# Mixer output projection: plain tiles against Strassen's seven half-size products

## Chip, cores and metric

One core of one Trainium2 chip (trn2) runs the whole kernel. The metric is device time in microseconds of one execution; the time before is 785.6 us, the median of three runs.

## What is computed

The reference is one layer of a hybrid decoder trunk on 512 tokens of width 1024. What matters here is the step that closes the token mixer, and its neighbours:

```python
h = rmsnorm(x, mix_norm)
z = h @ w_in
y_a = pool_mixer(z_pool, w_pool, pool_scale) @ w_branch_a
y_b = spatial_gating(z_uv, ...) @ w_branch_b
x = x + (sigmoid(z_gate_a) * y_a + sigmoid(z_gate_b) * y_b) @ w_out
h = rmsnorm(x, ffn_norm)
x = x + conv_ffn(h, w_up, conv_w, conv_b, w_down)
```

`w_out` is 1024 x 1024. The mixed operand, called `ga` in the kernel, is 512 x 1024, so the projection is 512 x 1024 times 1024 x 1024. The change rewrites this one product.

## The kernel before

**Three matmuls for one.** Every fp32 operand is cut into a rounded part and a rest, both in the type fp32r, and each product of a 128 x 128 and a 128 x 512 block is three matmuls: high by high, high by low, low by high (`mm3`, lines 201 to 205). Activations are cut by `split` (ScalarE copies the high part, VectorE subtracts the rest: lines 235 and 236). Weights are cut by `parts` (line 68 on ScalarE, line 69 on VectorE) from a raw block of 128 x 1024 that a DMA on SP's queue has loaded.

**Weights in a queue.** `plan` and `plan_seven` put units (a load and a cut) in the list `todo`. `take` (line 154) hands the next cut unit to the matmuls and first prepares further ones, so that two more stay ready (`AHEAD`), with loads up to four units further (`LOADS`). The cut pairs live in two rings of four buffers (`wp`). Raw weights, activations' pairs and the residual all share one pool of 37 blocks of 4 KB per partition (`blk`). Instructions are emitted in program order and then scheduled, so on an engine they may stand in another order than in the text.

**Two ways to multiply.** `by_token` (line 407) is the plain way: for one half `fh` of the output columns, four PSUM banks (one for each block of 128 tokens) collect the eight blocks of the contraction; a unit of weights serves 24 matmuls of 512 columns. `seven` (line 347) is Strassen's way, in Winograd's form: token halves, contraction halves and column halves give seven products instead of eight, each of 24 matmuls here, in two units of 12. Its stationary operands are the blocks A11, A12, A22 and four combinations D, S2, S3 and E. `combine` (line 333) makes these with four VectorE subtractions or additions of 256 columns, and `halves` and `cut_into` cut them. The weights' combinations are made in `plan_seven`: by VectorE on the raw block (`adds="vector"`), by accumulating DMAs on POOL's queue, or by both (`"some"`). Three sets of weights of the input projection and the down projection go this way already; the latter in three parts with the order `DOWN`.

**Around the change.** The branch product of `yp` with `w_a` runs by `by_token` for `fh` 0 and 1 (lines 571 to 576). After each half, VectorE multiplies the four banks by the gate (line 575) and adds `gb` (line 576); that gives `ga`. Then the residual `x` (line 581) and the embedding input `pt` (line 587) are loaded on ScalarE's DMA queue, and `pt` is split. Then TensorE turns all eight channel tiles of `ga`: four transposes of 128 x 128 per tile, through the identity, into one bank (`turned`, line 614), and each is split into `m`. `by_token(m, ...)` with `w_o` runs for both halves; VectorE adds the result to `x` (line 626) and ScalarE squares it (line 604). Then 24 matmuls embed `pt` (`embed`), while the norm (line 599 on POOL, line 649 on VectorE) is made, and TensorE turns the normed rows `xn` for the up projection.

Of the kernel before, what the change touches and what calls it, by code (L numbers as in the profile page):

```python
# [7 lines left out]
F32 = mybir.dt.float32  # L8
F32R = mybir.dt.float32r
AF = mybir.ActivationFunctionType  # L10
ALU = mybir.AluOpType
PSUM = bass.MemoryType.PSUM

P = 128
T = 512
H = T // 2
D = 1024
KD = D // P
NT = T // P
FF = 2816  # L20
KF = FF // P
# [5 lines left out]
AHEAD = 2  # L27
# [3 lines left out]
HK = KD // 2  # L31
# [3 lines left out]
DOWN = ("P1", "P5", "P2", "P6", "P7", "P4", "P3")  # L35
# [9 lines left out]
def trunk(ctx, tc, xT, xr, pT, wsT, par, bsp, w_u0, w_u1, w_v, w_ga, w_gb, w_p, w_pl,  # L45
# [6 lines left out]
    small = ctx.enter_context(tc.tile_pool(name="small", bufs=2))  # L52
# [4 lines left out]
    V, S, G, PE = nc.vector, nc.scalar, nc.gpsimd, nc.tensor  # L57

    def block(name, shape=(2, T), dtype=F32):
        return blk.tile([P, *shape], dtype, tag="blk", name=name)  # L60


    def parts(raw, cols=CW, first=False, spare=False):

        pool, th, tl = (blk, "blk", "blk") if spare else (wp, "hi", "lo")
        hi = pool.tile([P, CW], F32R, tag=th, name="whi")
        lo = pool.tile([P, CW], F32R, tag=tl, name="wlo")
        (V.tensor_copy if first else S.copy)(hi[:, :cols], raw[:, :cols])  # L68
        V.tensor_tensor(lo[:, :cols], raw[:, :cols], hi[:, :cols].bitcast(F32), op=ALU.subtract)  # L69
        return hi, lo  # L70
# [3 lines left out]
    todo = []  # L74
# [3 lines left out]
    def load_raw(src):  # L78
        raw = block("raw", (CW,))
        n = src.shape[-1]  # L80
        nc.sync.dma_start(raw[:, :n], src)
        return raw
# [5 lines left out]
    def plan(src, cols=CW, **kw):  # L88
        got = []
        todo.append((lambda: got.append(load_raw(src)), lambda: parts(got[0], cols, **kw)))  # L90
# [56 lines left out]
    def prepare(loads=LOADS):  # L147
        while todo and len(loaded) < loads:
            load, cut = todo.pop(0)
            load()  # L150
            loaded.append(cut)
        ready.append(loaded.pop(0)())

    def take(ahead=AHEAD, loads=LOADS):
        while (todo or loaded) and len(ready) <= ahead:
            prepare(loads)
        return ready.pop(0)

    flat = "p k f -> p (k f)"
# [19 lines left out]
            plan_map(i // 5)  # L179
    for i in range(KD):  # L180
        plan(w_a[i // 4, i % 4].rearrange(flat))
    for i in range(KD):
        plan(w_o[i // 4, i % 4].rearrange(flat))
    for k in range(2):
        plan(w_ple[k])
    done_at = {q0 + n: (q0, n) for q0, n in PARTS}
# [14 lines left out]
    def mm3(o, w, a, first, last, **kw):  # L201
        (wh, wl), (ah, al) = w, a
        PE.matmul(o, wh, ah, start=first, stop=False, **kw)  # L203
        PE.matmul(o, wh, al, start=False, stop=False, **kw)  # L204
        PE.matmul(o, wl, ah, start=False, stop=last, **kw)  # L205

    def wslice(c, j, n=P):
        return c[0][:, j * n:(j + 1) * n], c[1][:, j * n:(j + 1) * n]

    def act(b, sl=slice(None)):  # L210
        return b[:, 0, sl], b[:, 1, sl]

    def work(name):
        return tmp.tile([P, T], F32, tag="work", name=name, bufs=8)

    def bank():
        return ps.tile([P, T], F32, tag="mm", name="mm")
# [9 lines left out]
    def split(src, scale=None):  # L227

        b = block("blk", (2, T), F32R)
        split_into(b, src, scale)  # L230
        return b
# [18 lines left out]
    def col(c, i):  # L250
        return pr[:, c + i:c + i + 1]
# [9 lines left out]
    ident = const.tile([P, P], F32, name="ident")  # L261
# [59 lines left out]
    seeded = [psb.tile([P, T], F32, tag=f"sd{n}", name="sd") for n in range(2)]  # L321
# [82 lines left out]
        for f in fill:  # L404
            f()

    def by_token(acts, fh, banks, kps, between=None):

        for kp in kps:
            c = take()  # L410
            for b in range(NT):
                for kk in range(2):
                    k = 2 * kp + kk
                    mm3(banks[b], act(acts[k], slice(b * P, (b + 1) * P)), wslice(c, kk, T), k == 0, k == KD - 1)


    x2 = []
    x = []
# [12 lines left out]
    for k in range(KD):  # L431
        if k + 1 < KD:
            load(k + 1)
        b = split(x[k], col(C_MIX, k))
        c = take(1, 1)
# [87 lines left out]
    ga = gate(X, [nothing] * 3 + [(lambda f=f: head(f)) for f in range(HEADS)])  # L523
# [22 lines left out]
    yp = []  # L546
# [11 lines left out]
    for i in range(KD):  # L558
        pooled.append(pool(i))
        fh = i // 4  # L560
        if i % 4 == 0:
            banks = [bank(), bank(), *seeded]
# [5 lines left out]
            group_maps(i // 5)  # L568


    for fh in range(2):
        banks = [bank() for _ in range(NT)] if fh == 0 else [bank(), *seeded, bank()]
        by_token(yp, fh, banks, range(KD // 2))
        for b in range(NT):
            V.tensor_tensor(ga[b][:, fh], banks[b], ga[b][:, fh], op=ALU.mult)
            V.tensor_tensor(ga[b][:, fh], ga[b][:, fh], gb[b][:, fh], op=ALU.add)

    x = [block("x") for _ in range(NT)]
# [23 lines left out]
    def squares(b, fh, sums):  # L602
        sq = work("sq")
        S.activation(sq, x[b][:, fh], AF.Square, accum_out=sums[b][:, fh:fh + 1])

    def columns(z, b, f):

        return z[b][:, f // HK, f % HK * P:(f % HK + 1) * P]

    def turned(z, f):  # L610

        tp = bank()
        for b in range(NT):
            PE.transpose(tp[:, b * P:(b + 1) * P], columns(z, b, f), ident)  # L614
        return tp


    m = []
    for f in range(KD):
        m.append(split(turned(ga, f)))  # L620
    xss = [small.tile([P, 2], F32, tag="xss", name="xss", bufs=NT) for _ in range(NT)]
    for fh in range(2):
        banks = [bank() for _ in range(NT)] if fh == 0 else [*seeded, bank(), bank()]
        by_token(m, fh, banks, range(KD // 2))
        for b in range(NT):
            V.tensor_tensor(x[b][:, fh], banks[b], x[b][:, fh], op=ALU.add)
            squares(b, fh, xss)


    c_ple = [take(), take()]  # L630
# [30 lines left out]
    xss = [small.tile([P, 2], F32, tag="xss", name="xss", bufs=NT) for _ in range(NT)]  # L661
# [11 lines left out]
    for i in range(KF):  # L673
        if i:
            o1, o2 = proj8(xg), proj8(xg)
        else:

            o1, o2 = bank(), bank()
            c = [take(), take()]
# [3 lines left out]
        a = conv(2 * i, o1)  # L683
        S.activation(a, a, AF.Gelu)
        b = conv(2 * i + 1, o2)
        V.tensor_tensor(a, a, b, op=ALU.mult)
        if i % 2 == 0:
            q = i // 2
# [5 lines left out]
        else:  # L694
            z = split(a)
# [3 lines left out]
        if part:  # L699
            q0, n = part  # L700
# [31 lines left out]
    for b in (2, 3, 0, 1):  # L732
        th, j = divmod(b, 2)
# [9 lines left out]
        n = 0  # L743
        for group in groups:
            for k in range(KD):
                a = XE[th][k % HK][:, k // HK]
                a = [a[:, z, j * P:(j + 1) * P] for z in range(2)]
                for ob, c0 in group:
                    mm3(ob, a, [z[:, c0:c0 + ob.shape[-1]] for z in wg[k]], k == 0, k == KD - 1)
            for ob, c0 in group:  # L750
                w = ob.shape[-1]
                fh, c1 = divmod(c0, T)
# [22 lines left out]
def _layout(i):  # L775

    import numpy as np

    a = {k: np.asarray(v) for k, v in i.items()}

    def ft(w):
        K, F = w.shape
        return w.reshape(K // P, P, F // P, P).transpose(2, 1, 0, 3)

    def th(w):
        return w.reshape(KD // 2, 2, P, 2, T).transpose(3, 0, 2, 1, 4)

    def sv(w):
        return w.reshape(2, HK, P, 2, T).transpose(0, 3, 1, 2, 4).reshape(4, HK, P, T)

    def cols(v):
        return v.reshape(-1, P).T

    w_in = a["w_in"][0]
    up = ft(a["w_up"][0])
    cw, cb = a["conv_w"][0], a["conv_b"][0]

    def pairs(z):
        return np.stack([z[:KF], z[KF:]], 1).reshape(z.shape)

    cwt = pairs(cw.T.reshape(2 * KF, P, 3)).transpose(1, 0, 2).reshape(P, -1)
    cbt = pairs(cb.reshape(2 * KF, P)).T
    par = np.concatenate([cols(a["mix_norm"][0]), cols(a["pool_scale"][0]), cols(a["sgu_norm"][0]),
                          cols(a["ffn_norm"][0]), cols(a["ple_norm"][0]), cwt, cbt], 1)
    o = {
        "xT": a["x"][0].T.reshape(KD, P, T),
        "xr": a["x"][0].reshape(NT, P, D),
        "pT": a["p"][0, 0].T.reshape(2, P, T),
        "wsT": a["w_spatial"][0].transpose(2, 0, 1),
        "par": par,  # L810
        "bsp": a["b_spatial"][0],
        "w_u0": w_in[:, D:D + T].reshape(KD, P, T),
        "w_u1": ft(w_in[:, D + T:2 * D]),
        "w_v": sv(w_in[:, 2 * D:3 * D]),
        "w_ga": sv(w_in[:, 3 * D:4 * D]),
        "w_gb": sv(w_in[:, 4 * D:]),
        "w_p": ft(w_in[:, :D]),
        "w_pl": a["w_pool"][0].reshape(2, 2, 2, P, 256).transpose(0, 3, 1, 2, 4),
        "w_a": th(a["w_branch_a"][0]),
        "w_b": th(a["w_branch_b"][0]),  # L820
        "w_o": th(a["w_out"][0]),
        "w_up": pairs(up),

        "w_dn": a["w_down"][0].reshape(KF // 2, 2, P, 2, T).transpose(1, 3, 0, 2, 4).reshape(4, KF // 2, P, T),
        "w_g": a["w_ple_gate"][0].reshape(KD, P, D),
        "w_ple": a["w_ple"][0].reshape(2, P, D),
        "gfin": a["final_norm"],
    }
    return {k: np.ascontiguousarray(o[k]) for k in _ORDER}
# [14 lines left out]
```

## Time and profile before

| | before |
|---|---|
| median of 3 runs (lowest, highest) | 785.6 us (785.59, 786.09) |
| the profiled execution: its own time | 787.91 us |
| the profiled execution: span from first to last instruction | 786.2 us |
| TensorE busy | 771.4 us (98%) |
| VectorE busy | 547.2 us (70%) |
| ScalarE busy | 372.9 us (47%) |
| POOL busy | 42.8 us (5%) |
| DMA moved | 95.35 MB, 121 GB/s over the span |

Busy time of TensorE is modelled to the end of each matmul, and matmuls overlap, so the distance from start to start is what one costs. "PEld" is the loading of stationary weights, which runs beside the matmuls. A bracket behind a row gives the idle time just before it and what ended that. The chain that ended last is followed back from the last instruction, at each step to what released it.

### The profile page before, as it was taken

How to read it: one execution, taken by the hardware profiler on the slowest of the kernel's cores; microseconds unless marked ns; L12 is line 12 of the kernel's file. 1: busy time of each engine (PE TensorE's matmuls, PEld its weight loads, DVE VectorE, ACT ScalarE, POOL GpSimd, SP SyncE). 2: the span in 40 equal slices, each digit the busy share in tenths (PEclk: the TensorE clock that was granted, in tenths of full speed). 3: DMA queues.
4: the chain of work that ended last, by engine and by line, in shares of the span. 5: the costliest groups of instructions: out<-in, count | busy, mean ns of one | idle time of the engine just before them, and what ended most of it. 6: DMA issues, size and time to landing. Idle time of an engine off the chain costs nothing.

```text
span 786.2 us, 9275 instructions
## 1 busy us (share of the span) xinstructions
PE 771.4 (98%) x3482; PEld 637.8 (81%) x3482; DVE 547.2 (70%) x769; ACT 372.9 (47%) x538; POOL 42.8 (5%) x79
## 2 busy tenths in 40 slices
PE   9999999999999999999999999999999999999896
PEld 7888878888888888788888888888888888877785
DVE  7797898866576744536577678666668767788655
ACT  6576736582241322335544545534445434457623
POOL 0000200000112100001000010000000011000100
PEclk9999999999999999999999999999999999999999
DMA  9712225124031508102841344822425664310311
GB/s 350 270 55 81 80 81 188 54 103 166 28 127 62 214 29 324 49 0 76 325 103 37 102 108 132 289 91 51 108 82 133 232 170 111 117 54 31 130 55 54
DMA packets 36829, 95.35 MB, mean 121 GB/s; under 512 B 3376, under 2 KB 3504, under 8 KB 36784
## 3 DMA queue, kind: packets, MB, share of 16 engines
q1 hardware_dynamic: 32192, 84.68, 30.7%
q0 software_dynamic: 3008, 5.77, 4.7%
q10 hardware_dynamic: 1584, 4.31, 1.5%
q8 instruction: 27, 0.44, 0.2%
q14 instruction: 18, 0.15, 0.1%
HBM read 91.60 MB, written 3.15 MB: 121 GB/s over the span
## 4 chain that ended last, share of the span: by engine, by line
PE 89%; DVE 4%; DMA 2%; ACT 2%; issue 1%; POOL 0%; POOLq 0%; SPq 0%; ACTq 0%; DVEq 0%
PE mm L203 24%; PE mm L204 23%; PE mm L205 23%; PE sd L204 6%; PE sd L203 6%; PE sd L205 6%; DVE wlo L69 1%; ACT whi L68 1%; DMA pt<-in_pT 1%; DMA raw<-in_w_g 1%; PE mm L498 1%; DVE raw L137 1%; PE mm L614 0%; DMA x<-in_xT 0%; DVE xn L649 0%
## 5 line engine op out<-in xcount | busy, mean ns | idle before, releaser
L69 DVE TENSOR_TENSOR wlo<-raw,whi 128x1024 fp32r<-128x1024 f32 (+1 forms) x186 | 217.9, 1179 | 158.2 <-ACT whi L68 157.8
L68 ACT CAST whi<-raw 128x1024 fp32r<-128x1024 f32 (+1 forms) x179 | 183.7, 1031 | 214.7 <-PE mm L204 56.8
L203 PE MATMUL mm<-blk,whi 128*128 128x512 f32 x480 | 186.4, 390 | 0.6 <-ACT blk L238 0.6
L204 PE MATMUL mm<-blk,whi 128*128 128x512 f32 x480 | 186.7, 389 | 0.0
L205 PE MATMUL mm<-blk,wlo 128*128 128x512 f32 x480 | 186.6, 389 | 0.0
L203 PEld LDWEIGHTS mm<-blk,whi 128*128 128x128 f32 x480 | 90.0, 188 | 19.9 <-ACT blk L238 0.7
L205 PEld LDWEIGHTS mm<-blk,wlo 128*128 128x128 f32 x480 | 90.1, 188 | 18.9
L204 PEld LDWEIGHTS mm<-blk,whi 128*128 128x128 f32 x480 | 90.1, 188 | 18.5
L203 PE MATMUL mm<-whi,blk 128*128 128x512 f32 x214 | 83.7, 391 | 1.4 <-DVE xe L239 1.4
L204 PE MATMUL mm<-wlo,blk 128*128 128x512 f32 x214 | 83.4, 390 | 0.0
L205 PE MATMUL mm<-whi,blk 128*128 128x512 f32 x214 | 83.3, 389 | 0.0
L203 PEld LDWEIGHTS mm<-whi,blk 128*128 128x128 f32 x214 | 40.2, 188 | 10.1 <-issue 1.8
L205 PEld LDWEIGHTS mm<-whi,blk 128*128 128x128 f32 x214 | 40.2, 188 | 8.4
L204 PEld LDWEIGHTS mm<-wlo,blk 128*128 128x128 f32 x214 | 40.2, 188 | 8.1
L203 PE MATMUL sd<-whi,blk 128*128 128x512 f32 x110 | 43.1, 392 | 0.3 <-ACT u L367 0.3
L204 PE MATMUL sd<-wlo,blk 128*128 128x512 f32 x110 | 42.8, 389 | 0.0
L205 PE MATMUL sd<-whi,blk 128*128 128x512 f32 x110 | 42.8, 389 | 0.0
L137 DVE TENSOR_TENSOR raw<-raw 128x1024 f32<-128x1024 f32 (+1 forms) x36 | 42.0, 1199 | 0.1
L203 PE MATMUL sd<-whi,cmb 128*128 128x512 f32 x92 | 36.2, 395 | 0.8 <-ACT u L367 0.8
L204 PE MATMUL sd<-wlo,cmb 128*128 128x512 f32 x92 | 36.1, 392 | 0.8 <-DVE wlo L69 0.8
L205 PE MATMUL sd<-whi,cmb 128*128 128x512 f32 x92 | 35.8, 389 | 0.0
L205 PE MATMUL mm<-whi,cmb 128*128 128x512 f32 x92 | 35.8, 389 | 0.0
(167 smaller groups left out, 1047.9 us busy)
## 6 DMA issues: line engine op xcount, KB each, us to landing
raw<-in_w_up SPq DMA_DIRECT2D x44, 512.0 KB, 4.3
raw<-in_w_dn SPq DMA_DIRECT2D x25, 512.0 KB, 3.5
raw<-in_w_dn POOLq DMA_DIRECT2D x10, 512.0 KB, 6.0
raw<-in_w_v SPq DMA_DIRECT2D x8, 512.0 KB, 11.3
raw<-in_w_ga SPq DMA_DIRECT2D x8, 512.0 KB, 4.0
raw<-in_w_gb SPq DMA_DIRECT2D x8, 512.0 KB, 3.7
raw<-in_w_p SPq DMA_DIRECT2D x8, 512.0 KB, 4.7
raw<-in_w_b SPq DMA_DIRECT2D x8, 512.0 KB, 3.9
```

The costliest lines, as they stand in the source:

```text
L68: (V.tensor_copy if first else S.copy)(hi[:, :cols], raw[:, :cols])
L69: V.tensor_tensor(lo[:, :cols], raw[:, :cols], hi[:, :cols].bitcast(F32), op=ALU.subtract)
L137: V.tensor_tensor(z[:, :cols], z[:, :cols], raw[extra, ch][:, :cols], op=ALU.add)
L203: PE.matmul(o, wh, ah, start=first, stop=False, **kw)
L204: PE.matmul(o, wh, al, start=False, stop=False, **kw)
L205: PE.matmul(o, wl, ah, start=False, stop=last, **kw)
L498: PE.matmul(mx[:, n * P:(n + 1) * P], vt[n].rearrange("p a t -> p (a t)")[:, f * P:(f + 1) * P], wsm[:, f, :], start=True, stop=True)
```

## The change

The output projection goes by `seven`, with the accumulating DMAs making all the weights' combinations (`adds="all"`) and the cut units of the products P1 and P5 placed in the block pool instead of the rings (`spare`). The operand is turned by pairs of channel tiles (`turn_pair`): two tiles are transposed into two banks, one is copied to SBUF, and the blocks and combinations for one contraction step are made from both. Pairs 0 and 1, which need only the first half of `ga`, are turned after the second and third unit of the second half of the branch product; pairs 2 and 3 after it. There, `take` keeps three, then four units ready instead of two. `w_o` is laid out like `w_dn`.

```diff
-    for i in range(KD):
-        plan(w_o[i // 4, i % 4].rearrange(flat))
+    todo.extend(plan_seven(blocks(w_o), DOWN, "all", spare=("P1", "P5")))
...
-    def by_token(acts, fh, banks, kps, between=None):
-
+    def by_token(acts, fh, banks, kps, ahead=AHEAD, after=()):
+
+        after = list(after)
         for kp in kps:
-            c = take()
+            c = take(ahead)
             for b in range(NT):
                 for kk in range(2):
                     k = 2 * kp + kk
                     mm3(banks[b], act(acts[k], slice(b * P, (b + 1) * P)), wslice(c, kk, T), k == 0, k == KD - 1)
+            if after:
+                after.pop(0)()
...
+    m = []
+    m11 = []
+
+    def turn_pair(q):
+        tp, s2 = turned(ga, 2 * q), turned(ga, 2 * q + 1)
+        s1 = work("s1")
+        S.copy(s1, tp)
+        if q % 2 == 0:
+            m11.append(block("a11", (2, 2, H), F32R))
+        t = m11[-1][:, q % 2]
+        cut_into(t, s1[:, :H])
+        z = split(s2)
+        m.append(dict(A11=t, A12=z[:, :, :H], A22=z[:, :, H:], **combine(s1, s2)))
+
     for fh in range(2):
         banks = [bank() for _ in range(NT)] if fh == 0 else [bank(), *seeded, bank()]
-        by_token(yp, fh, banks, range(KD // 2))
+        early = [nothing, lambda: turn_pair(0), lambda: turn_pair(1)] if fh else ()
+        by_token(yp, fh, banks, range(KD // 2), 3 + fh, early)
         for b in range(NT):
             V.tensor_tensor(ga[b][:, fh], banks[b], ga[b][:, fh], op=ALU.mult)
             V.tensor_tensor(ga[b][:, fh], ga[b][:, fh], gb[b][:, fh], op=ALU.add)
...
-    m = []
-    for f in range(KD):
-        m.append(split(turned(ga, f)))
+
+    for q in (2, 3):
+        turn_pair(q)
     xss = [small.tile([P, 2], F32, tag="xss", name="xss", bufs=NT) for _ in range(NT)]
-    for fh in range(2):
-        banks = [bank() for _ in range(NT)] if fh == 0 else [*seeded, bank(), bank()]
-        by_token(m, fh, banks, range(KD // 2))
-        for b in range(NT):
-            V.tensor_tensor(x[b][:, fh], banks[b], x[b][:, fh], op=ALU.add)
-            squares(b, fh, xss)
+
+    def drain_m(th, j, fh, src):
+        b = 2 * th + j
+        V.tensor_tensor(x[b][:, fh], src, x[b][:, fh], op=ALU.add)
+        squares(b, fh, xss)
+
+    seven(m, drain_m, DOWN)
...
+    def alt(w):
+        n = w.shape[0] // P // 2
+        return w.reshape(n, 2, P, 2, T).transpose(1, 3, 0, 2, 4).reshape(4, n, P, T)
...
-        "w_o": th(a["w_out"][0]),
+        "w_o": alt(a["w_out"][0]),
```

## Rows read from the trace of the kernel before

**Rows 1.** The page: busy time by engine, then the chain that ended last.

```profile
PE 771.4 (98%) x3482; PEld 637.8 (81%) x3482; DVE 547.2 (70%) x769; ACT 372.9 (47%) x538; POOL 42.8 (5%) x79
...
PE 89%; DVE 4%; DMA 2%; ACT 2%; issue 1%; POOL 0%; POOLq 0%; SPq 0%; ACTq 0%; DVEq 0%
```

**Rows 2.** Stretches: length, busy PE, PEld, DVE, ACT, POOL, clock, DMA share, GB/s.

```profile
314.90:320.40 5.50, 4.90 (x35) 3.65 (x33) 5.50 (x10) 4.66 (x8) 0.00 (x0) 1.00 0.36 141
320.40:342.40 22.00, 22.00 (x97) 18.22 (x98) 9.16 (x13) 5.66 (x11) 0.00 (x0) 1.00 0.00 1
```

**Rows 3.** Timeline of PE: output projection's first and last matmul, turning after the embedding.

```profile
320.32 0.50 PE L203 MATMUL mm<-whi,blk 128*128 128x512 f32 x1
...
363.75 0.39 PE L205 MATMUL mm<-whi,blk 128*128 128x512 f32 x1
...
369.42 4.56 PE L614 MATMUL mm<-ident,xn 128*128 128x128 f32 x32
```

**Rows 4.** Timeline of PE: end of the branch product, turning of `ga`.

```profile
314.91 0.39 PE L205 MATMUL mm<-whi,blk 128*128 128x512 f32 x1
315.14 2.51 PE L614 MATMUL mm<-ident,sg 128*128 128x128 f32 x19
317.92 0.33 PE L614 MATMUL mm<-ident,sg 128*128 128x128 f32 x1 [0.27 <-DVE sg L576]
318.52 1.85 PE L614 MATMUL mm<-ident,sg 128*128 128x128 f32 x12 [0.27 <-DVE blk L236]
```

**Rows 5.** Timeline of PE: first part of the down projection (`seven`), first matmul; the next work.

```profile
472.04 0.39 PE L203 MATMUL mm<-whi,a 128*128 128x512 f32 x1
...
510.12 0.39 PE L203 MATMUL mm<-blk,whi 128*128 128x512 f32 x1
```

**Rows 6.** Timeline of PE: third part of the down projection, first matmul; the turning behind it.

```profile
689.64 0.39 PE L203 MATMUL mm<-whi,a 128*128 128x512 f32 x1
...
720.20 1.03 PE L711 MATMUL mm<-ident,x 128*128 128x128 f32 x8
```

**Rows 7.** Timeline of ACT and its DMA queue during the branch product's second half.

```profile
299.06 1.05 ACT L68 CAST whi<-raw 128x1024 fp32r<-128x1024 f32 x1 [4.43 <-PE mm L205]
299.54 1.13 ACTq L587 DMA_DIRECT2D pt<-in_pT  x2
308.50 0.62 ACT L235 CAST blk<-pt 128x512 fp32r<-128x512 f32 x1 [8.38 <-DMA pt<-in_pT]
```

**Rows 8.** Timeline of DVE from the wait for `pt` to the splits of `m`.

```profile
309.15 0.69 DVE L236 TENSOR_TENSOR blk<-pt,blk 128x512 fp32r<-128x512 f32 x1 [7.78 <-ACT blk L235]
...
312.98 0.68 DVE L575 TENSOR_TENSOR sg<-mm,sg 128x512 f32<-128x512 f32 x1
...
316.58 1.28 DVE L576 TENSOR_TENSOR sg<-sg 128x512 f32<-128x512 f32 x2
317.79 4.87 DVE L236 TENSOR_TENSOR blk<-mm,blk 128x512 fp32r<-128x512 f32 x8
```

**Rows 9.** Groups by line, 522 to 530 us (feed-forward): the work for one contraction step.

```profile
L331 DVE TENSOR_TENSOR cmb<-d,cmb 128x512 fp32r<-128x512 f32 x1 | 0.7, 685 | 0.0
...
L337 DVE TENSOR_TENSOR d<-cc 128x256 f32<-128x256 f32 x1 | 0.4, 425 | 0.0
```

**Rows 10.** DMA issues (KB each, median us to landing), then POOL's timeline.

```profile
raw<-in_w_dn POOLq DMA_DIRECT2D x10, 512.0 KB, 6.0
...
470.02 1.20 POOL L105 DMA_DIRECT2D raw<-in_w_dn  x1 [6.54 <-DVE cmb L331]
```

**Rows 11.** Timeline of PE in the closing gate product, then a stretch as in rows 2.

```profile
739.99 0.50 PE L203 MATMUL mm<-whi,xe 128*128 128x512 f32 x1 [1.23 <-ACT whi L68]
741.25 0.74 PE L204 MATMUL mm<-wlo,xe 128*128 128x512 f32 x1 [0.76 <-DVE wlo L69]
...
742.00:744.70 2.70, 2.70 (x7) 2.12 (x7) 2.37 (x6) 1.12 (x3) 0.00 (x0) 0.50 0.00 0
```

**Rows 12.** Timeline of DVE at the end of the norm behind the output projection.

```profile
368.45 1.68 DVE L649 TENSOR_SCALAR xn<-x,fr 128x512 f32<-128x512 f32 x4 [0.52 <-POOL fr L599]
```

More of the change, by code (lines that the diff above doesn't have):

```diff
@@ L568, in trunk, with columns, turned @@
             group_maps(i // 5)
+    def columns(z, b, f):
+        return z[b][:, f // HK, f % HK * P:(f % HK + 1) * P]
+    def turned(z, f):
+        tp = bank()
+        for b in range(NT):
+            PE.transpose(tp[:, b * P:(b + 1) * P], columns(z, b, f), ident)
+        return tp
+    m = []
[10 more added lines that the diff above has]
+        m.append(dict(A11=t, A12=z[:, :, :H], A22=z[:, :, H:], **combine(s1, s2)))
     for fh in range(2):
         banks = [bank() for _ in range(NT)] if fh == 0 else [bank(), *seeded, bank()]
-        by_token(yp, fh, banks, range(KD // 2))
+        early = [nothing, lambda: turn_pair(0), lambda: turn_pair(1)] if fh else ()
+        by_token(yp, fh, banks, range(KD // 2), 3 + fh, early)
         for b in range(NT):
@@ L604, in squares @@
         S.activation(sq, x[b][:, fh], AF.Square, accum_out=sums[b][:, fh:fh + 1])
[L606 to L612, printed above, removed]
-        for b in range(NT):
-            PE.transpose(tp[:, b * P:(b + 1) * P], columns(z, b, f), ident)
-        return tp
-    m = []
-    for f in range(KD):
-        m.append(split(turned(ga, f)))
-    xss = [small.tile([P, 2], F32, tag="xss", name="xss", bufs=NT) for _ in range(NT)]
-    for fh in range(2):
-        banks = [bank() for _ in range(NT)] if fh == 0 else [*seeded, bank(), bank()]
-        by_token(m, fh, banks, range(KD // 2))
-        for b in range(NT):
-            V.tensor_tensor(x[b][:, fh], banks[b], x[b][:, fh], op=ALU.add)
-            squares(b, fh, xss)
+    for q in (2, 3):
+        turn_pair(q)
+    xss = [small.tile([P, 2], F32, tag="xss", name="xss", bufs=NT) for _ in range(NT)]
+    def drain_m(th, j, fh, src):
[3 more added lines that the diff above has]
+    seven(m, drain_m, DOWN)
     c_ple = [take(), take()]
@@ L820, in _layout @@
         "w_b": th(a["w_branch_b"][0]),
-        "w_o": th(a["w_out"][0]),
+        "w_o": alt(a["w_out"][0]),
         "w_up": pairs(up),
-        "w_dn": a["w_down"][0].reshape(KF // 2, 2, P, 2, T).transpose(1, 3, 0, 2, 4).reshape(4, KF // 2, P, T),
+        "w_dn": alt(a["w_down"][0]),
         "w_g": a["w_ple_gate"][0].reshape(KD, P, D),
```

## The prediction

> **What bounds the kernel now.** I read the page's busy times first, then its chain. TensorE is busy for 98% of the span, and 89% of the chain that ended last is TensorE's [rows 1]; the reader is to see that only fewer or shorter matmuls, or shorter waits of TensorE, can move the time. Next the stretches. While the output projection runs, the clock is granted at 1.00 (2.4 GHz), VectorE is busy for 9.16 of 22 us and the DMA share is 0.00: this stage is pure TensorE. While `ga` is turned it is not: there VectorE is busy for all of 5.50 us and TensorE for 4.90 [rows 2]. So the change has to be judged in two places: the matmuls that it saves, and VectorE's work around the turning. The timeline gives the spacing. The plain product's 192 matmuls start from 320.32 to 363.75 us, 43.43 us for 191 steps, 0.227 each [rows 3]. A product of the same size by seven is in this trace already, the first part of the down projection: 168 matmuls in 510.12 - 472.04 = 38.08 us, 0.2267 each and no gap [rows 5].
>
> **Matmuls removed.** 24 of 192, at 0.2267 us: -5.44 us, all on TensorE's path.
>
> **Transposes.** There are 32 before and after. In a row without waits 32 take 4.56 us [rows 3], 0.1425 each, so moving 16 into the branch product saves and costs nothing by itself; that product then starts its last matmul at 314.91 + 2.28 = 317.19 instead of 314.91 [rows 4]. What changes is the wait. Now it is 320.32 - 314.91 - 0.23 - 4.56 = 0.62 us, short because sixteen transposes of the first half stand there while VectorE finishes the second half of `ga` [rows 4]. Afterwards these sixteen are gone from that place. The earliest end of the last block's gate: 317.19, the matmul's 0.39, one multiply and one add (1.28 for two such operations [rows 8]): 318.86. TensorE can do three transposes (blocks 0 to 2 of one tile) until 317.19 + 0.23 + 0.43 = 317.85. So the wait is at least 1.0 us if it keeps program order; below that only if P1's matmuls, whose first operands come from pairs 0 and 1, are put in front. That the scheduler can reorder shows on VectorE, where two additions of line 576 stand in a row though the text alternates lines 575 and 576 [rows 8].
>
> **VectorE's and ScalarE's extra work.** For a pair VectorE does three operations of 512 columns (0.61 us from start to start: eight take 4.87 [rows 8]) and five of 256 at 0.42 [rows 9]: 3.9 us. Four pairs are 15.7 us in place of 4.87, and six more weight cuts add some 7 us. All of it lies beside 45 us of TensorE work in a stage where VectorE is less than half busy [rows 2], so I cost the sum at nothing; its cover is thin in one place only, the two pairs turned during the branch product. There VectorE waits until 309.15 for the split of `pt` and is then busy without a pause until the last addition ends at 317.79 [rows 8]. The cause is in front: ScalarE stands at its split for 8.38 us until `pt` lands, and that transfer was issued at 299.54, behind a cut that had waited 4.43 us for TensorE to free a ring buffer [rows 7]. If `pt` still stands in front of the pairs on ScalarE's queue, the two pairs' 7.8 us come on top of the 8.64. Two things shorten this. The cuts at this point now go to the block pool, so they don't wait for TensorE: up to some 2.5 us earlier for `pt`. And two cuts of about 1.1 us can be done before that time. With both, the gate ends at 317.79 + 7.8 - 2.5 - 2.3 = 320.8, and the wait is 320.8 - 317.85 = 2.95. I take the middle of 1.0 and 2.95, 2.0 us: +1.4 over now.
>
> **Weights.** SP issues 10 loads instead of 8. POOL issues 8 accumulating DMAs, 1.20 us each on POOL, 6.0 from issue to landing by the down projection's [rows 10]. A block t is loaded, then added to three times: for P5, after P5's cut for P6, after P6's cut for P4. From a cut to the next cut of the same block there are at least three units of 12 matmuls, 8.2 us, against 6.0, and cuts run two units ahead. During the projection the DMA share is 0.00 [rows 2], so there is room. Queued behind POOL's waits is only the norm's power (line 599), which comes after the last cut. Cost nothing; above, half of one such landing, 3 us, if a raw block comes late because the 37 blocks are full; below, nothing to gain, since TensorE doesn't wait for weights here.
>
> **Copies and drains in the product.** The first down part ran without a gap [rows 5]. The third took 720.20 - 689.64 = 30.56 us for 126 matmuls [rows 6], 2.0 more than 126 times 0.2267, its operands also made just in front of it. I take 0, since here no weight is added on VectorE and none is cut while P1 runs; bound +2.0.
>
> **End of the stage.** After the last product VectorE owes two blocks a subtraction and an addition, then the norm: 0.68 twice, scalings 1.68 and POOL's 0.52 [rows 8, 12], 3.6 us and about 1 for the squares, against 369.42 - 363.75 = 5.67 that the embedding covers [rows 3]. Nothing; above 1.1, a weight cut in between.
>
> **Sum.** -5.44 + 1.4 = -4.0. The profiled execution has 787.91 us (span 786.2 and 1.7 around it), which would be 783.9; it stands 2.3 above the median of the runs, 785.6, so for the runs: 785.6 - 4.1 = 781.5.
>
> **A rule against it.** In the closing product TensorE stood for 1.23 and 0.76 us within 3 us, and the next 2.70 us had a granted clock of 0.50, 1.2 GHz [rows 11]: some 1.4 us lost. Around the turning, with 0.62 us of waits, it stayed at 1.00 [rows 2]. My wait of 2.0 us in one piece is near the first case; at the same loss the forecast would be 782.9, which is inside the range. The Trainium skill ("TensorE: Matmul & The Clock Gate", section "Part 4: PE-mode transpose") says that transposes don't count as activity that keeps the clock up; by it the clock would have dropped in the 5.4 us of turning before, and the rows show that it did not. By that rule the matmuls behind the turning would already run at half clock now, and turning less in one place would give some of that back; with nothing to give back, the sum stays.
>
> **Rivals.**
> - *VectorE late at the turning (slower side).* `pt` lands as late as now, ScalarE's order keeps it ahead of the pairs, and nothing is done earlier. The gate ends at 317.79 + 7.8 = 325.6, TensorE waits 7.75 instead of 0.62, and the clock falls as in rows 11: +7.1 + 1.4 - 5.44 = +3.1, so 788.7. It decides from the time at which VectorE starts again: at 309.15 it is slower by that much, at 306.0 the gain is just eaten, at 304.4 it is still 1.6 faster. For it: the queue orders in rows 7 and 8, and more DMA traffic. Against it: the earlier issue. Chance 0.11 beyond +0.2%, and 0.14 for the part between, near 785.
> - *The product itself is paced as in rows 6.* 2.0 us of waits at the handing over of banks and cuts: 783.5. Chance 0.12.
> - *The early turning doesn't take place*, because banks aren't free and the scheduler leaves all transposes together. Then the wait is near 0.62 as now and the matmuls are still saved: 785.6 - 5.4 = 780.2. Chance 0.08.
> - *The forecast*, 781.5, with waits at the turning between 0 and 3 us (780 to 783): chance 0.55.
>
> **How the numbers follow.** A difference of 0.2% (1.6 us) is about what measuring this kernel can tell from none. Faster beyond it holds the forecast, the pacing and the unmoved turning: 0.75. Within it, the part of the VectorE case near break-even: 0.14. Slower: 0.11. The range takes in no wait at all at the turning (785.6 - 5.44 - 0.62 = 779.5) below, and above the VectorE case up to 786.0, where about 0.15 is left out.
>
> **What would show it.** Right: 24 fewer matmuls on lines 203 to 205 each less eight (page), 0.2267 us spacing in the product, two groups of eight transposes inside the branch product, a wait of 1 to 3 us in front of the last transposes that ends with VectorE's line for the gate, clock 1.00 in the stage. Wrong: a wait over 4 us at the turning with clock 0.50 behind it; PE rows released by line 69 or by an accumulating DMA within the product; or waits in the embedding.

## The result, and the profile after

The changed kernel takes 810.53 us, median of four runs (809.39 to 812.32), against 785.6 before (785.58 to 786.09): ratio 1.0318, 95% interval 1.0302 to 1.0333. It is 24.9 us slower. The prediction said 781.5 us, with 779.5 to 786.0 as its range: a gain where the change lost. The profiled execution took 810.04 us, its span is 808.3.

Lines have moved: matmuls stand at L202 to L204, the turning at L581, the copy in the turning at L590, the gate at L603 and L604, the loads of `x` and `pt` at L609 and L615, the casts of blocks and cuts at L234, L329 and L68, the norm's scaling at L666.

First the page's busy times and traffic, after (answers to [rows 1]), then TensorE's waits between 300 and 400 us (engine, line, releaser: us in total, times, longest).

```profile
PE 770.3 (95%) x3458; PEld 636.1 (79%) x3458; DVE 566.5 (70%) x803; ACT 388.3 (48%) x562; POOL 52.5 (7%) x87
...
DMA packets 40574, 100.59 MB, mean 124 GB/s; under 512 B 3537, under 2 KB 3665, under 8 KB 40529
```

```profile
PE mm L202 <- ACT a L329: 16.5, 1, 16.5
PE mm L581 <- DVE sg L604: 4.9, 1, 4.9
PE mm L581 <- DVE xn L666: 1.1, 1, 1.1
PE mm L581 <- DVE blk L238: 1.0, 1, 1.0
PE mm L202 <- ACT s L590: 0.6, 1, 0.6
```

The 24 matmuls are gone and TensorE is less of the span, 95% for 98. One wait alone is 16.5 us, and it ends with ScalarE. TensorE's timeline, after (answers to [rows 3, 4]):

```profile
305.10 1.03 PE L581 MATMUL mm<-ident,sg 128*128 128x128 f32 x8
...
311.43 1.03 PE L581 MATMUL mm<-ident,sg 128*128 128x128 f32 x8
...
317.78 0.60 PE L581 MATMUL mm<-ident,sg 128*128 128x128 f32 x4
...
323.28 1.11 PE L581 MATMUL mm<-ident,sg 128*128 128x128 f32 x4 [4.90 <-DVE sg L604]
...
347.48 0.80 PE L202 MATMUL mm<-whi,a 128*128 128x512 f32 x1 [16.48 <-ACT a L329]
348.07 0.63 PE L203 MATMUL mm<-wlo,a 128*128 128x512 f32 x1
...
390.55 0.71 PE L581 MATMUL mm<-ident,xn 128*128 128x128 f32 x5
```

The two early groups of eight transposes are where the prediction wanted them. Behind the long wait the matmuls start 0.42 to 0.43 us apart, not 0.227. The stretches say why (columns: stretch, length, busy time of PE, PEld, DVE, ACT, POOL, then the granted clock, DMA share and GB/s):

```profile
320.00:330.00 10.00, 6.05 (x21) 4.54 (x22) 8.06 (x16) 2.42 (x4) 2.38 (x2) 0.66 0.55 139
330.00:340.00 10.00, 0.99 (x5) 0.47 (x3) 1.23 (x1) 0.22 (x1) 3.65 (x3) 0.75 1.02 315
340.00:350.00 10.00, 2.52 (x6) 2.06 (x7) 3.51 (x8) 3.12 (x7) 0.00 (x0) 0.50 1.09 291
350.00:360.00 10.00, 10.00 (x41) 8.14 (x41) 5.09 (x11) 3.55 (x7) 0.00 (x0) 0.90 1.03 354
```

After 16.5 us without work TensorE runs at 0.50, 1.2 GHz. And the DMA share, 0.00 in this stage before [rows 2], is full for 30 us. What TensorE waits for is on ScalarE's timeline (answers to [rows 7]):

```profile
294.41 1.06 ACT L68 CAST whi<-raw 128x1024 fp32r<-128x1024 f32 x1 [4.38 <-PE mm L204]
...
318.60 1.04 ACT L68 CAST whi<-raw 128x1024 fp32r<-128x1024 f32 x1 [2.69 <-DMA raw<-in_w_o]
319.55 0.61 ACT L329 CAST cmb<-e 128x512 fp32r<-128x512 f32 x1
...
325.72 1.95 ACTq L609 DMA_DIRECT2D x<-in_xr  x4
327.78 0.86 ACTq L615 DMA_DIRECT2D pt<-in_pT  x2
...
343.77 0.62 ACT L234 CAST blk<-pt 128x512 fp32r<-128x512 f32 x1 [13.55 <-DMA pt<-in_pT]
346.50 0.62 ACT L234 CAST blk<-pt 128x512 fp32r<-128x512 f32 x1 [2.11 <-DMA pt<-in_pT]
347.02 0.40 ACT L329 CAST a<-s 128x256 fp32r<-128x256 f32 x1
```

`pt` is loaded at 327.78, not at 299.54 [rows 7]; its split stands on ScalarE in front of the cut `a` of pair 2, and ScalarE works in order. So a tile that is not needed before the embedding, some 40 us later, holds the product. The same mechanism makes the wait before it: the cut at 318.60 waits for an accumulating load (issued at 312.71, 5.87 us to landing in the chain that ended last), behind it stands pair 1's last block at 319.55, behind that the gate. VectorE's and GpSimd's timelines:

```profile
320.20 0.69 DVE L330 TENSOR_TENSOR cmb<-e,cmb 128x512 fp32r<-128x512 f32 x1 [2.80 <-ACT cmb L329]
...
325.54 0.33 DVE L243 COPY x<-sg 128x1 f32<-128x1 f32 x4
325.79 0.20 DVE L243 COPY pt<-sg 128x1 f32<-128x1 f32 x2
```

```profile
312.71 1.19 POOL L105 DMA_DIRECT2D raw<-in_w_o  x1 [42.67 <-DVE wlo L69]
```

The small copies at 325.54 open the loads of `x` and `pt`; they run only behind the last gate. GpSimd had stood idle for 42.67 us in front of the accumulation issued at 312.71, until a cut ended it.

**The account by the traces.** The first part of the down projection starts at 495.38 for 472.04 [rows 5], 23.3 later, 0.8 of it older than the stage (the small product near 100 us starts at 100.43 for 99.60). The other 22.5: -5.4 for the matmuls; +21.4 of waits (16.5, 4.9 and 0.6 against 0.54 in [rows 4]); +2.2 between the norm's first transpose and the down projection (104.83 us against 102.62); which leaves 4.3, and the clock explains that much: the stretches price it as busy time times what is missing of the clock, 6.05 x 0.34 + 0.99 x 0.25 + 2.52 x 0.50 + 10 x 0.10 = 4.6. (The spans differ by 22.1 only, since the profiled execution before stood 2.3 above its median, for a stall near its end.)

### The profile page after: what moved, and what is told of

It is laid out like the page before. It is cut to its first block, busy times and chain, and to the rows that moved or that the text cites. A ratio compares the mean times of both kernels' runs of the same rounds, so it can differ in the third digit from the quotient of the medians.

```text
span 808.3 us, 9310 instructions
## 1 busy us (share of the span) xinstructions
PE 770.3 (95%) x3458; PEld 636.1 (79%) x3458; DVE 566.5 (70%) x803; ACT 388.3 (48%) x562; POOL 52.5 (7%) x87
## 2 busy tenths in 40 slices
DMA packets 40574, 100.59 MB, mean 124 GB/s; under 512 B 3537, under 2 KB 3665, under 8 KB 40529
## 4 chain that ended last, share of the span: by engine, by line
PE 80%; DMA 6%; issue 6%; DVE 5%; ACT 2%; POOL 1%; SPq 0%; POOLq 0%; ACTq 0%; DVEq 0%
PE mm L202 21%; PE mm L203 20%; PE mm L204 20%; PE sd L203 6%; PE sd L202 6%; PE sd L204 6%; DMA raw<-in_w_o 2%; DMA pt<-in_pT 2%; DVE wlo L69 2%; ACT whi L68 1%; DMA raw<-in_w_g 1%; PE mm L500 1%; DVE raw L137 1%; DMA x<-in_xT 0%; DVE xn L666 0%
## 5 line engine op out<-in xcount | busy, mean ns | idle before, releaser
L69 DVE TENSOR_TENSOR wlo<-raw,whi 128x1024 fp32r<-128x1024 f32 (+1 forms) x192 | 225.0, 1181 | 139.3 <-ACT whi L68 138.6
L68 ACT CAST whi<-raw 128x1024 fp32r<-128x1024 f32 (+1 forms) x185 | 189.8, 1032 | 198.1 <-PE mm L203 57.6
L202 PE MATMUL mm<-blk,whi 128*128 128x512 f32 x480 | 187.1, 392 | 0.2 <-ACT blk L237 0.2
L204 PE MATMUL mm<-blk,wlo 128*128 128x512 f32 x480 | 186.6, 389 | 0.0
L202 PEld LDWEIGHTS mm<-blk,whi 128*128 128x128 f32 x480 | 90.5, 189 | 19.4 <-ACT blk L237 0.5
L204 PEld LDWEIGHTS mm<-blk,wlo 128*128 128x128 f32 x480 | 90.1, 188 | 18.9
L202 PE MATMUL mm<-whi,blk 128*128 128x512 f32 x174 | 68.2, 392 | 1.4 <-DVE xe L238 1.4
L203 PE MATMUL mm<-wlo,blk 128*128 128x512 f32 x174 | 67.8, 390 | 0.0
L204 PE MATMUL mm<-whi,blk 128*128 128x512 f32 x174 | 67.7, 389 | 0.0
L203 PE MATMUL sd<-wlo,cmb 128*128 128x512 f32 x108 | 42.3, 392 | 0.8 <-DVE wlo L69 0.8
L202 PE MATMUL sd<-whi,cmb 128*128 128x512 f32 x108 | 42.4, 394 | 0.8 <-ACT u L366 0.8
L202 PE MATMUL mm<-whi,cmb 128*128 128x512 f32 x108 | 42.3, 391 | 0.0
L203 PE MATMUL mm<-wlo,cmb 128*128 128x512 f32 x108 | 42.3, 391 | 0.0
L204 PE MATMUL sd<-whi,cmb 128*128 128x512 f32 x108 | 42.0, 389 | 0.0
L204 PE MATMUL mm<-whi,cmb 128*128 128x512 f32 x108 | 42.0, 389 | 0.0
L202 PE MATMUL sd<-whi,blk 128*128 128x512 f32 x102 | 40.0, 392 | 0.3 <-ACT u L366 0.3
L204 PE MATMUL sd<-whi,blk 128*128 128x512 f32 x102 | 39.7, 389 | 0.0
L202 PEld LDWEIGHTS mm<-whi,blk 128*128 128x128 f32 x174 | 32.7, 188 | 8.3 <-issue 1.8
```

## The experiments

Three theories were stated first. **A**: the order is to blame, twice: buffers of the block pool go out in program order, so what stands behind the early pairs in the program is loaded late, and ScalarE then waits in order for it. **B**: the ten loads and eight accumulating loads saturate the transfers. **C**: the 37 blocks run out.

Runs 1, 2 and 4 to 8 are single executions; the kernels that were timed more often spread over 1.7 to 3.5 us, so differences of 1 or 2 us between single runs say nothing.

**1. `pt` early** (e1): load and split in front of the branch product, in the program and so on ScalarE's queue.

```diff
+    pp = []
+    for k in range(2):
+        pt = work("pt")
+        later(pt[:, :1], gb[0][:, 0, :1])
+        nc.scalar.dma_start(pt, pT[k])
+        pp.append(act(split(pt)))
     for fh in range(2):
...
-    pp = []
-    for k in range(2):
-        pt = work("pt")
-        later(pt[:, :1], ga[0][:, 0, :1])
-        nc.scalar.dma_start(pt, pT[k])
-        pp.append(act(split(pt)))
```

> Only the load and the split of pt are moved, to the place before the branch product's loop (waiting for gb instead of ga). Theory A (the split of pt stands on ScalarE's queue in front of pair 2's blocks, and pt is issued late because its buffer, like x's blocks, is handed out in program order behind the early pairs): the wait of 16.5 us in front of P1 goes, the wait of 4.9 us at the turning stays, clock 1.00 again; 788 to 793 us. Theory B (the added accumulating DMAs saturate the transfers, so everything that lands in this stage is late): the wait moves to another transfer (x or a raw block) and the time stays above 800. Theory C (the 37 blocks are full): two blocks held longer make it no better, 808 or more.

Measured 800.84 us (before on the same chip: 785.40). The 16.5 us are gone, as A says, yet only 9.7 us come back: A's 788 to 793 did not come, and B had named what did, a wait that moves to a raw block and a time above 800. TensorE's waits, then ScalarE's timeline, of this run:

```profile
PE sd L202 <- ACT u L366: 8.6, 1, 8.6
PE mm L581 <- DVE sg L611: 4.6, 1, 4.6
```

```profile
324.65 1.92 ACTq L616 DMA_DIRECT2D x<-in_xr  x4
...
349.97 1.05 ACT L68 CAST whi<-raw 128x1024 fp32r<-128x1024 f32 x1 [13.53 <-DMA raw<-in_w_o]
```

A second wait of the same kind, which the first had covered: a cut whose weights are still being accumulated stands 13.53 us in front of the drain copies `u`, for whose bank TensorE waits.

**2. `x` and `pt` between the halves** (e2): both loads go into the loop over `fh`, behind the first half's gate, so ahead of the pairs.

```diff
             V.tensor_tensor(ga[b][:, fh], ga[b][:, fh], gb[b][:, fh], op=ALU.add)
+        if fh == 0:
+            x = [block("x") for _ in range(NT)]
+            for b in range(NT):
+                later(x[b][:, 0, :1], ga[0][:, 0, :1])
+                nc.scalar.dma_start(x[b].rearrange("p a t -> p (a t)"), xr[b])
+            pp = []
...
```

> The loads of x and pt and pt's split are moved between the two halves of the branch product, so in program order they stand ahead of the early pairs. Theory A: x is issued at about 294 us again as before the change instead of 325.7, pt lands before 312, the 16.5 us go; ScalarE may wait for pt in front of pair 0 instead, so 785 to 793 us. Theory B: x and pt still land late, beside the accumulating DMAs, over 800. Theory C: x can't get its blocks before the second half ends, so it is issued after 315 and the time stays over 800.

Measured 800.88 us, where B had it and not A. But `x` is issued at 294.17 us again, as A said, `pt`'s split waits 8.20 and 2.20 us as in [rows 7], and the waits are 5.7 for the gate and 7.8 for `u`. So the place in the program decides when these loads go out.

**3. All pairs after the product** (e3, run once, then timed): `early = ()` and `for q in range(4)` behind the loop.

> All four pairs are turned after the branch product; the seven products stay. Theory A: x and pt are issued at about 294 us as before the change, no wait for pt in front of P1; in its place TensorE waits for the pairs' work on VectorE and ScalarE (four pairs of 3.9 us, of which P1 needs the first part): 4 to 8 us of waits, 784 to 790 us. Theory B: still a long wait for a transfer, over 800. Theory C: the pairs' fourteen blocks come later, so x is issued early and the time falls as in theory A.

> The kernel that turns all four pairs after the branch product, timed. The waits of TensorE in its stage are about 2.5 us more at the turning and 2 more at the norm than before, against 5.4 saved, so theory A expects a ratio of 0.998 to 1.001 to the kernel before. Theory B (the seven products themselves, or their transfers, are slower than the plain product) expects above 1.002.

Measured 788.06 in the first run (expected by A: 784 to 790) and 788.01 (786.88 to 789.66) in six timed runs against 785.49 in eleven: ratio 1.0031, interval 1.0019 to 1.0043. `x` is issued at 298.9 us, and neither long wait is there (the longest is 1.8). 22.5 of the 24.9 us hang on the half of the turning that was put forward; yet without it the change still loses a little. A's ratio of 0.998 to 1.001 was missed, and 1.0031 lies on B's side. The trace names the loss, and it is not the products themselves: 3.1 us of waits at the turning for 0.54, 2.2 at the norm, and a clock that falls in front of the product, here from 325 to 330 us (columns as above); from 330 us on the clock is 1.00.

```profile
325.00:330.00 5.00, 5.00 (x14) 3.84 (x13) 4.70 (x12) 3.83 (x8) 0.52 (x1) 0.55 1.10 247
```

**4. No spare blocks** (e5): P1's and P5's cuts go to the rings.

```diff
-    todo.extend(plan_seven(blocks(w_o), DOWN, "all", spare=("P1", "P5")))
+    todo.extend(plan_seven(blocks(w_o), DOWN, "all"))
```

> P1's and P5's cut weights go to the rings of four instead of the block pool, which frees eight of the 37 blocks. Theory C: x is issued before 305 us and the wait for pt goes, below 795. Theory A: x still stands behind pair 1's blocks in the order in which blocks are handed out, so it is issued after 312; the wait for pt stays above 8 us, the time above 798. Theory B: no change beyond 3 us.

Measured 802.53 us, 8 less than the change. With those blocks left to the pool `x` still goes out at 323.2 us and TensorE waits 8.6 us for pair 2's `a`. C's signs (`x` before 305 us, a time below 795) did not come, and B's (no change beyond 3 us) did not either. The 8 us go with the transfers: from 323 to 349 us GpSimd issues no accumulation here, and `pt` lands in 10.2 us (median), not 17.1.

That blocks go out in program order is my reading of runs 2, 3 and 4, and it is not shown. The copies that open the loads of `x` stand on VectorE right behind the last gate, with no idle time before them, in the changed kernel (325.54) and here (323.00). Their place in VectorE's own order would delay the loads as well, and no run separates the two. What is shown is that the loads come late when they stand behind the early pairs in the program, and early when they don't.

**5 and 6. The second wait from two sides.** e6: run 1, and VectorE adds the weights (`"vector"` for `"all"`), so that no load accumulates. e7: run 1, accumulating loads kept, but the weights are cut earlier and `x` is loaded behind pair 3:

```diff
-        by_token(yp, fh, banks, range(KD // 2), 3 + fh, early)
+        by_token(yp, fh, banks, range(KD // 2), 3 + 4 * fh, early)
```

> As the kernel with pt loaded early, but the weights' combinations are made by VectorE on the raw blocks, with no accumulating DMA. Theory A2 (with pt out of the way, what is left are cuts on ScalarE's queue that wait for accumulating DMAs, which themselves wait for P5's cut, whose block stands behind pair 0's blocks in the order of handing out): both waits of the kernel with pt early (4.6 at the turning, 8.6 in front of P7) go or fall below 2 us each; 784 to 789 us. Theory B2 (VectorE and ScalarE are simply too late with the pairs): eight more additions of 1.2 us on VectorE make the wait at the turning longer than 4.6, and the time stays above 797.

> As the kernel with pt loaded early, accumulating DMAs kept; the second half of the branch product keeps seven units ready instead of four, so P5's cuts and the loads behind them stand ahead of the early pairs in program order, and x's loads stand behind pairs 2 and 3. Theory A2: P5 is cut before 300 us, its accumulating DMAs are issued before 302 and not at 312, the wait of 4.6 at the turning and that of 8.6 in front of P7 go; 784 to 790. Theory B2: no change, 798 to 802. Theory C (blocks run out): the pairs wait for blocks instead, and the waits move to the turning, over 795.

Measured 786.82 and 786.92 us, 14 less than run 1. The wait in front of P7 is gone in both; that at the turning is 2.5 us in e6 (A2: below 2). TensorE's waits of e7 from 300 to 400 us, and one line of GpSimd's timeline:

```profile
PE mm L581 <- DVE sg L611: 1.9, 2, 1.7
PE mm L581 <- DVE xn L667: 1.1, 1, 1.1
PE mm L581 <- DVE blk L238: 1.0, 1, 1.0
PE mm L202 <- ACT s L590: 0.3, 1, 0.3
```

```profile
295.39 1.19 POOL L105 DMA_DIRECT2D raw<-in_w_o  x1 [16.22 <-DVE wlo L69]
```

Plain saturation (B) is out: e7 moves the same 100.59 MB. What counts, as I read it, is when an accumulation can start. A block's next accumulation waits for its cut; in the changed kernel P5's cuts come behind pair 0's blocks, from 310 us, in e7 seven units are kept ready, and GpSimd's accumulations go on at 295.39 instead of 312.71. But e7 holds two edits: `x` goes out at 331.88 us instead of run 1's 324.65 too, so the earlier cuts alone are not shown to give the 14 us. One line of DMA issues (250 to 400 us) from each of the changed kernel, run 1 and e7, in this order (last column: median us to landing):

```profile
raw<-in_w_o POOLq DMA_DIRECT2D x8, 512.0 KB, 11.1
```

```profile
raw<-in_w_o POOLq DMA_DIRECT2D x8, 512.0 KB, 10.0
```

```profile
raw<-in_w_o POOLq DMA_DIRECT2D x8, 512.0 KB, 7.8
```

The prediction took 6.0 [rows 10]. The Trainium skill ("DMA: Bandwidth & Descriptors", section "Anatomy of one DMA — SWDGE (gpsimd) path") fits 2.0 us plus bytes over 436 GB/s to this path, an estimate of 3.2 us for 512 KB; the medians here, accumulating and under load, are 2.4 to 3.5 times that.

**7. VectorE's additions alone** (e12): the changed kernel with `"vector"`, `pt` where it was.

> The changed kernel, pt loaded and split where the change has it, with the one edit that VectorE adds the difference weights and no load accumulates. Theory A (pt's split stands ahead of pair 2 on ScalarE's queue and pt is issued near 325 us because buffers come in program order): x's and pt's loads are issued near 325 us still, and TensorE waits behind the split again; without the accumulating loads beside it pt lands in 8 to 10 us instead of 16 to 18, so the wait is 6 to 10 us and the time 793 to 800. Rival B2 (the accumulating loads alone made both waits, and pt's place is harmless without them): no wait over 3 us in front of the output projection, and the time is that of the run with pt early and VectorE's additions, 786.8.

Measured 797.85 us, with waits of 9.3 us for `a` and 2.6 for the gate (TensorE's longest wait, then ScalarE's timeline):

```profile
PE mm L202 <- ACT a L329: 9.3, 1, 9.3
```

```profile
333.48 0.62 ACT L234 CAST blk<-pt 128x512 fp32r<-128x512 f32 x1 [7.22 <-DMA pt<-in_pT]
```

A again; the B2 of this run, the accumulations alone, falls. (The B2 in runs 5 and 6 is another rival.) With the runs before it makes a square:

| | accumulating loads | VectorE adds |
|---|---|---|
| `pt` behind the pairs | 810.5 | 797.9 |
| `pt` early | 800.8 | 786.8 |

The two faults are nearly independent: 10 to 11 us for `pt`'s place, 13 to 14 for the accumulations.

**8. Late turning, VectorE adds** (e8): run 3 with `"vector"`.

> As the kernel that turns all pairs after the branch product, with VectorE making the weights' combinations and no accumulating DMA. Theory A2: there were no waits for accumulating DMAs in it, so nothing to gain; eight more VectorE operations of 1.2 us within 38 us of the product: 0 to 2 us slower than the kernel with all pairs turned after, 786 to 790. Theory B2: VectorE is the bound at the turning; 2 to 5 us slower.

Measured 785.39 us, no change against before, below both forecasts and 2.6 below run 3. Much of that is the clock: from 325 to 330 us e8 starts 23 matmuls at 0.98, run 3's two profiled executions 17 at 0.70 and 14 at 0.55, which is 6 or 9 times 0.227, 1.4 or 2.0 us.

**9 to 11. What is left at the norm.** In each run above TensorE still waits 1.1 for `xn` and 1.0 for `blk`, the 2.2 us of the account. VectorE's timeline of e7:

```profile
361.75 1.28 DVE L370 TENSOR_TENSOR u<-mm,u 128x512 f32<-128x512 f32 x2
362.94 1.28 DVE L642 TENSOR_TENSOR x<-u,x 128x512 f32<-128x512 f32 x2
364.15 1.22 DVE L69 TENSOR_TENSOR wlo<-raw,whi 128x1024 fp32r<-128x1024 f32 x1
...
366.13 1.67 DVE L667 TENSOR_SCALAR xn<-x,fr 128x512 f32<-128x512 f32 x4 [0.63 <-POOL fr L623]
...
368.71 1.67 DVE L667 TENSOR_SCALAR xn<-x,fr 128x512 f32<-128x512 f32 x4 [0.58 <-POOL fr L623]
```

The product by seven ends with blocks 0 and 1 (361.75), and the norm begins with them; blocks 2 and 3, which that drain doesn't touch, come second. Theory N puts the norm in the order 2, 3, 0, 1:

```diff
-    for b in range(NT):
+    for b in (2, 3, 0, 1):
         r = rstd_1([xss[b][:, 0:1], xss[b][:, 1:2]])
```

in e9 (on e7), e10 (on e8) and e11 (on e7, with VectorE's additions), all timed together.

> The early turning stays, pt and the P5 and P1 weights are wanted ahead as in the runs before, the accumulating loads stay; new is that the norm in front of the up projection takes the blocks in the order 2, 3, 0, 1, in which P3's drain leaves blocks 0 and 1 to the end. Theory N (the norm of all four blocks stands behind the last drain because VectorE does block 0's first; TensorE's waits of 1.1 for xn and 1.0 for blk are that): both waits together fall from 2.1 to 1.1 or less, and the time from 786.9 to 785 to 786, about the kernel before. Rival D (the last drain itself, a subtraction, an addition and the squares behind them, ends last, whatever order follows): both waits stay at 2.1 and the time at 786.9.

> All four pairs are turned after the branch product, the difference weights are added by VectorE (785.4 in the look before), and the norm takes blocks 2, 3, 0, 1. Theory N: the waits for xn and blk fall from 2.1 to 1.1 or less and the time to 783.5 to 784.5, faster than before by 0.15 to 0.25%. Rival D: both waits stay and the time is 785.4, no change against before.

> The early turning, pt and the weights wanted ahead, the difference weights added by VectorE and no accumulating load, the norm in the order 2, 3, 0, 1. Theory A2 (what the early turning lost was late buffers and cuts behind late accumulating loads, and nothing else): with both gone the early turning is no worse than the late one, 783.5 to 785. If the early turning costs by itself (VectorE and ScalarE reach pair 1's blocks after TensorE wants them): a wait of 1.5 to 3 us for sg at the second turning stays and the time is 1 us or more above the run with all pairs turned after the product.

| run | median us (12 runs) | lowest to highest | ratio to before (785.26, 29 runs) |
|---|---|---|---|
| e9 | 784.63 | 783.74 to 785.40 | 0.9988 (0.9979 to 0.9996) |
| e10 | 785.40 | 784.31 to 787.82 | 0.9998 (0.9986 to 1.0010) |
| e11 | 784.06 | 782.90 to 786.35 | 0.9981 (0.9971 to 0.9992) |

In all three the two waits fall from 2.1 to 0.8, and from the norm's first transpose to the down projection it is 103.0 us for 104.8: N holds. In e9 VectorE now does three of the four scalings of blocks 2 and 3 before the last drain (TensorE's wait, then VectorE's timeline):

```profile
PE mm L581 <- DVE xn L667: 0.8, 2, 0.5
```

```profile
359.17 1.28 DVE L667 TENSOR_SCALAR xn<-x,fr 128x512 f32<-128x512 f32 x3 [0.60 <-POOL fr L623]
...
361.49 1.28 DVE L370 TENSOR_TENSOR u<-mm,u 128x512 f32<-128x512 f32 x2
```

e11 came out as expected, though the wait of 1.9 us for `sg`, which its rival named, stayed. e9's waits fell as expected; its time is 0.4 below the 785 forecast. e10 missed: 783.5 to 784.5 was expected, 785.40 measured, as much as e8's single run. The stretches of e8, e10 and e11 show it, each 320 to 330 us:

```profile
320.00:325.00 5.00, 3.45 (x11) 2.63 (x12) 4.70 (x12) 3.47 (x8) 0.00 (x0) 0.67 0.57 202
325.00:330.00 5.00, 5.00 (x23) 4.15 (x22) 4.97 (x11) 3.80 (x9) 0.00 (x0) 0.98 0.82 302
```

```profile
320.00:325.00 5.00, 3.03 (x10) 2.31 (x11) 4.70 (x12) 3.04 (x6) 0.00 (x0) 0.69 0.46 170
325.00:330.00 5.00, 5.00 (x16) 3.94 (x15) 4.97 (x12) 3.51 (x8) 0.00 (x0) 0.63 0.61 232
```

```profile
320.00:325.00 5.00, 4.57 (x24) 3.12 (x23) 5.00 (x7) 1.94 (x4) 0.00 (x0) 1.00 0.06 11
325.00:330.00 5.00, 5.00 (x23) 3.98 (x22) 4.96 (x13) 3.03 (x7) 0.00 (x0) 1.00 0.90 310
```

With all 32 transposes in one place and 2.8 us of waits among them and behind them the clock falls, in e8 until 325 and in e10 until past 328 us, with the same waits. From 325 to 330 e10 starts 16 matmuls where e8 starts 23: that is 7 x 0.227 = 1.6 us, about what N had given (1.8).

The granted clocks of the timed executions say the same. Six of e10's twelve have 0.996 or 0.997 and took 784.3 to 785.1 us; the other six have 0.992 to 0.994 and took 785.7 to 787.8. The profiled one (786.11) is of the second kind.

## Why the prediction was wrong

- *Matmuls removed*: right. 24 fewer, 0.227 apart where the clock is full. (The sum takes 4.1 off where its terms give 4.0; it should read 781.6.)
- *Transposes*: right but for sizes. Two groups of eight, and with the two faults mended TensorE waits 1.9 us at the turning (2.5 in e6), where the text took 2.0. Eight transposes take 0.79 us (305.10 to the next matmul at 305.89), 0.10 each and not the 0.1425 that was taken. Four switches from transposes to matmuls, where there was one, cost some 0.1 each (the first matmul's successor starts 0.33 behind it, not 0.227), which I had not counted.
- *VectorE's and ScalarE's extra work*: **the step that failed.** It read rightly that `pt`'s split blocks ScalarE and that its load stood behind a cut that waited for a ring buffer, and then assumed that the change would bring the load forward "up to some 2.5 us", because the cuts no longer wait for TensorE. The cuts at this place still waited 4.38 us for TensorE (294.41 above), and the load came 28 us later (327.78 for 299.54), behind the early pairs and the last gate, because it stands behind them in the program (run 2); whether through buffers or through VectorE's order is open. ScalarE's queue was taken as a cover for more work; its order was the risk.
- *Weights*: **failed too.** "Cost nothing; above 3 us" measured 13 to 14. The step priced each accumulation alone, 6.0 us against 8.2 between cuts, with the transfers idle. It did not ask when the first one that waits for a cut can start: that cut itself stands behind pair 0 on ScalarE, so at 312.71. From there the rest came close together, with `x` and `pt`, into a DMA share over 1.0.
- *Copies and drains in the product*: right; in e11 no gap is in it.
- *End of the stage*: mis-sized. Nothing was taken, 1.1 the bound; it is 2.2. The last drain was priced as two operations of 0.68; it is four, 2.4 us (361.75 to 364.15 in e7). The cut that the bound named does stand behind it (364.15), but it stands there in e9 too (363.89), where the waits are 0.8: the order of the norm's blocks was what the sum lacked.
- *The slower rival* (`pt` in front of the pairs on ScalarE, 788.7) had the mechanism and the side right. It put the split in front of pairs 0 and 1, a wait of 7.75 us; it stood in front of pair 2, and the wait was 16.5. Its condition "nothing is done earlier" was too kind: it was later.
- *The rule against it*: the price was 1.4 us for a wait of 2.0 in one piece. The changed kernel's waits of 4.9 and 16.5 left 4.3 for the clock. At about the predicted wait e7's clock fell (0.66 in 320 to 325 us, the row below) while e9's and e11's stayed at 1.00, and e6's too, with 2.5 us in one piece. The Trainium skill ("TensorE: Matmul & The Clock Gate", section "Part 4: PE-mode transpose") has transposes not count for the clock. The kernel before does not agree, 32 at 1.00 [rows 2]; e8 and e10, whose clock fell, had 2.8 us of waits beside their 32 and cannot tell one from the other.

```profile
320.00:325.00 5.00, 4.66 (x18) 3.57 (x18) 3.02 (x5) 0.49 (x1) 1.20 (x1) 0.66 0.89 236
```

**Where the rest of the gain went.** Even e11, with each fault mended, gains 1.2 us in the medians, not 4. Its profiled execution, 782.90, is the lowest of its runs and 2.4 below before's median. By its trace the down projection starts 2.5 us earlier against the small product near 100 us: -5.4 for the matmuls, +2.0 for TensorE's waits (turning 1.9, `s` 0.3, the norm's first transpose 0.3, against 0.54), +0.3 for the switches, +0.4 at the norm, -2.7 in sum. (The cheaper transposes, some 0.5, are not in it, so a few tenths stay unexplained.) Its other runs are up to 3.5 us slower, and their granted clocks go with that: the seven at 0.997 to 0.999 took 782.9 to 784.4 us, the five at 0.994 or 0.995 took 784.0 to 786.4; before, all 29 have 0.997 to 0.999. So part of the gain is lost to the clock in some executions. That it falls at the turning there is not shown, since only one execution of e11 is profiled.

## What to carry to other kernels

Before work is moved forward, list what then stands *behind* it in the program: loads, with the small instructions that open them, and on each in-order engine the unrelated instructions that wait for those loads; here one late transfer in front of a cast held TensorE for 16.5 us, three times what the change saved. A chain of loads that accumulate has to be priced from its first possible start, not by one transfer's duration. And a saving of 5 us at the bound engine is worth only as much as the consumer's order lets through: here the norm had to take its blocks as the new product finishes them.

## What was not expected of the hardware

- A load that lands in 2.6 us when it is issued ahead of the branch product (`pt` in e1, median) takes 17.1 (median) in the changed kernel, issued into the accumulations and the loads of `x`, and 10.4 in e12 without accumulations.
- Equal waits of TensorE, 1.7 us and 0.24 us at the turning, left the clock at 1.00 in e9 and e11 and at 0.66 for 320 to 325 us in e7; e6's single wait of 2.5 us left it at 1.00. Run 3's two executions, one kernel with the same waits (1.8, 1.0 and 0.3 us), had 0.70 and 0.55 from 325 to 330 us. Waits alone, as the trace gives them, do not tell which.
